# Seven products of quarters for the mixer's gate tiles in a float32 decoder step

## The chip, the cores and the metric

The kernel runs on one core of a Trainium2 chip. The metric is the device time of one execution in microseconds; the number for a kernel is the median of its runs.

## What is computed

One layer of a decoder over 560 token columns: 512 prompt tokens, 32 sampled tokens (8 sequences of 4) and 16 meta tokens. It is a feed-forward part, a mixer with two branches (gated linear attention and stick-breaking attention), and a second feed-forward part. The change is in the end of the mixer, cut here to what matters:

```python
u = rms_norm(h, mix_pre_g)
proj = u @ w_in                       # ..., r_a, q_b, k_b, v_b, gate_a, gate_b
o_a = rms_norm(o_a, gla_norm_g).reshape(B, L, V_GLA) * jax.nn.silu(r_a)
o_b = sb_attend(q_b, keys, vals, sb_bias, q_off).reshape(B, L, SB_W)
m = jax.nn.sigmoid(gate_a) * (o_a @ w_o_gla) + jax.nn.sigmoid(gate_b) * (o_b @ w_o_sb)
h = h + rms_norm(m @ w_out, mix_post_g)
```

All widths here are 1024, so each of `r_a`, `gate_a`, `gate_b` and the two output products has eight tiles of 128 output features. Everything is float32.

## The kernel before

Activations lie transposed: features on the 128 partitions, tokens along the free dimension, 544 tokens in this part, in two halves of 280 and 264 columns. A float32 product is made of float32r matmuls: an operand x is split into `hi`, its cast, and `lo`, x - hi, and a product takes three matmuls, hi·hi, hi·lo and lo·hi. A plain tile (`tile_steps`) goes over eight blocks of 128 input features and both halves of the tokens: 48 matmuls. After each six of them it yields once; such a step is the clock of the schedule.

Weights come by DMA in raw tiles of 128 x 1024 (three buffers). `split` has ScalarE cast one to `hi`, and `later(3, ...)` has VectorE subtract to `lo` three steps on (three buffers each). All vector subtractions and additions go through the one line L143. `later(n, f)` runs f after n more steps; `when` puts f at a given step. The order in which instructions are issued on TensorE, VectorE, ScalarE and GpSimd is that of the program, and each engine works through its own queue in that order. Temporary tiles come from an arena of 150 units of 280 columns (`take`, `give`), which reuses the room that has been free longest.

In the feed-forward parts most tile pairs (gate and up of one block of features) already take another form, `seven`: weights and activations are cut into quarters and the pair is made of seven products of quarters, after Strassen, instead of eight. Each product is 4 blocks x 3 matmuls of 272 columns, in all 84 matmuls and 14 steps. It takes four differences of weight quarters (`weight_sums`, 128x512), the parts of these (`parted`, `parted_lo`), four sums of activation quarters, made once, and five additions on the outputs.

In the mixer before, after the attention's own products, tiles follow each other in this order: r3 to r7 (`gate_r`, the silu gate of linear attention, whose results are split as they come), then for n = 0 to 7 an a tile (`gate_s`: the sigmoid of gate_a) and an o tile (`out_a`: o_a @ w_o_gla, multiplied by the sigmoid), then b0 to b7 (`gate_s` for gate_b), then p0 to p7 (o_b @ w_o_sb, `mixed`: times the sigmoid, plus m1, split for the next product), then the output projection m @ w_out, with halves of the tokens one after the other. Beside r3 to a4 run the products of the sampled tokens' attention; their last copies (`sample_out`) come at a4. The names and lines that matter below: `gate_s` L1940, `out_a` L1951, `names` L2067, `mixed` L2117, the loop over p L2144, the splits of the attention output at the second step of each b tile. At the start of each tile `ahead` splits the weights two tiles on and asks for a further raw tile; the hidden state, kept in DRAM meanwhile, is asked for at p1.

Of the kernel before, what the change touches and what calls it, by code (L numbers as in the profile page):

```python
# [8 lines left out]
F32 = mybir.dt.float32  # L9
# [6 lines left out]
P = 128  # L16
# [20 lines left out]
UP1 = (2, 5)  # L37
UP2 = (2, 5)
RE_FFN = 3
AHEAD = 150  # L40
SPREAD = 15
UNITS = 150
# [2 lines left out]
class Arena:  # L45
# [47 lines left out]
    def give(self, *aps):  # L93
        for a in aps:
            _, c, s, k = self.held.pop(id(a))
            self.clock += 1
            self.freed[c][s : s + k] = [self.clock] * k


class Parts:  # L100


    def __init__(self):
        self.t, self.rooms = {}, []

    def get(self, k, h, w):
        hi, lo = self.t[k, h]
# [4 lines left out]
def hybrid_step(  # L112
# [29 lines left out]
    def tt(out, a, b, op, eng=None):  # L142
        (eng or V).tensor_tensor(out=out, in0=a, in1=b, op=op)  # L143
# [683 lines left out]
    def gate_up_weights(plan, g_, u_, f0):  # L827
        for f in range(f0, KF):
            if f < RE_FFN or plan[f - RE_FFN] == "R":
                st.todo.extend((w, 0, KD, P * f, P, f < RE_FFN and "tile") for w in (g_, u_))  # L830
            else:
                st.todo.extend((w, r0, KD, P * f, P, "quarters") for w, r0 in (((g_, u_), 0), ((u_, g_), 4 * P)))

    def early_tiles(u, rs, wid, nw, hid, pairs, wait, prepare, first=False):

        early, held = {}, {}
# [39 lines left out]
    def other_tiles(old, gain, rs, nw, wid, hid, pairs, plan, late, sums_at, begun):  # L876
# [5 lines left out]
        QW = nw // 2  # L882
        QS = (slice(0, QW), slice(QW, nw))
        ub, sums = Parts(), {}
        pr_, ur, sr_, sp_ = {}, {}, {}, {}
        kinds = {RE_FFN + i: c for i, c in enumerate(plan)}
        start_, n = {}, 0
# [6 lines left out]
        def when(n, f, *args):  # L894
            at.setdefault(n, []).append((f, args))
# [59 lines left out]
            when(SP0 + SPE * i + 9, lambda i=i: give(pr_[i], pr_[i + 2]))  # L955


        quarters = {}

        def parted(f, key, src, room=None):  # L960

            count[0] += 1
            kt = src.shape[1]
            hi, lo = (sp.tile([P, KD, P], F32R, tag=t, name=f"{t}{count[0]}") for t in ("hi", "lo"))
            S.copy(hi[:, :kt], src)  # L965
            quarters[f, key] = hi, lo, src, room

        def parted_lo(f, key, more=False):
            hi, lo, src, room = quarters[f, key]
            tt(lo[:, : src.shape[1]], src, hi[:, : src.shape[1]].bitcast(F32), ALU.subtract)  # L970
            if room is not None:
                give(room)
            if more:
                st.fetch()

        def weight_sums(f, n):

            if n == 0:
                quarters[f] = st.raws.pop(0)[0], st.raws.pop(0)[0], take(KD * P), take(4 * P)
            r1, r2, t, t4 = quarters[f]  # L980
            t, t4 = (x.rearrange("p (k n) -> p k n", n=P) for x in (t, t4))
            b11, t1, b22, b21, t2, t3 = r1[:, :4], r1[:, 4:], r2[:, :4], r2[:, 4:], t[:, :4], t[:, 4:]
            tt(*((t3, b22, t1), (t1, t1, b11), (t2, b22, t1), (t4, b21, t2))[n], ALU.subtract)

        def parts_of(f, key):
            r1, r2, t, t4 = quarters[f]
            if key == "b1":
                parted(f, key, r1)
            elif key == "b2":
                parted(f, key, r2)  # L990
            elif key == "t":
                parted(f, key, t.rearrange("p (k n) -> p k n", n=P), t)
            else:
                parted(f, key, t4.rearrange("p (k n) -> p k n", n=P), t4)

        def raw_of(f, what):
            parted(f, what, st.raws.pop(0)[0])

        for f, c in kinds.items():
            n = start_[f]  # L1000
            if c == "S":
                for i, d in enumerate((-10, -10, -9, -8)):
                    when(n + d, weight_sums, f, i)
                for key, d, e in (("b1", -6, -5), ("t", -2, -1), ("b2", 0, 1), ("t4", 4, 6)):
                    when(n + d, parts_of, f, key)
                    when(n + e, parted_lo, f, key, key in ("b1", "b2"))
# [136 lines left out]
    st.todo += [(w, 0, KD, c + P * n, P, False) for n in range(8) for w, c in ((win, C_GA), (w_o_gla[0], 0))]  # L1143
    st.todo += [(win, 0, KD, C_GB + P * n, P, False) for n in range(8)]
    st.todo += [(w_o_sb[0], 0, KD, P * n, P, False) for n in range(8)]
# [4 lines left out]
    with tc.manual_schedule(engines={E.PE, E.DVE, E.Activation, E.Pool}):  # L1150
# [765 lines left out]
    def ahead():  # L1916
        st.split()
        st.fetch()
# [18 lines left out]
        later(2, by)  # L1937
        later(4, lambda: split(oas, n, o, oap))

    def gate_s(n, kept):  # L1940
        acc = yield from tile_steps(um, W1)
        sg = take(NW)
        kept.append(sg)

        def sig():
            for h in range(2):
                S.activation(sg[:, h * HW : h * HW + W2[h]], acc[h][:, : W2[h]], AF.Sigmoid)

        later(1, sig)

    def out_a(n):  # L1951
        acc = yield from tile_steps(oas, W1)

        def by():
            for h in range(2):
                c = slice(h * HW, h * HW + W2[h])
                tt(m1[n][:, c], acc[h][:, : W2[h]], m1[n][:, c], ALU.mult)

        later(1, by)

    def unwide():
        while wide:
# [23 lines left out]
    with tc.manual_schedule(engines={E.PE, E.DVE, E.Activation, E.Pool}):  # L1986
# [80 lines left out]
        names = [f"r{n}" for n in range(3, 8)] + [f"{c}{n}" for n in range(8) for c in "ao"] + [f"b{n}" for n in range(8)]  # L2067
        at = {}

        def when(t, n, f, *args):  # L2070

            at.setdefault(8 * names.index(t) + n, []).append((f, args))

        when("r4", 1, sample_new, 0)
        for i, t in enumerate(PAGES):
            if not t:
                continue
            what, c, b0 = t
            t = names[i]
            if what == "k":  # L2080
                for n, k in enumerate((1, 2, 5, 6)):
                    when(t, k, use_keys, b0, n)
                when(t, 9, sample_products, 1, b0, 0, kT, z)
                when(t, 9, sample_products, 1, b0, 1, kT, z)
            else:
                when(t, 1, use_values, c, b0)
            when(t, 7, ask)
        w1 = Weights(1)
        for n, f in w1.pieces(1):
            when("o1", n, f)  # L2090
        when("o1", 11, lambda: give(*qz, kns, z))
        when("a2", 5, sample_new, 1)
        t = names[len(PAGES)]
        when(t, 1, lambda: give(*ring))
        for n in range(4):
            when(t, 1 + 2 * n, sample_out, n)
        for n in range(8):
            when(f"b{n}", 2, lambda n=n: split(obs, n, ob[n], obp))
        mains = {f"r{n}": gate_r(n) for n in range(3, 8)}
        for n in range(8):  # L2100
            mains |= {f"a{n}": gate_s(n, m1), f"o{n}": out_a(n), f"b{n}": gate_s(n, sgb)}
        n = 0
        for t in names:
            ahead()
            for _ in mains[t]:
                n += 1
                step()
                for f, args in at.get(n, ()):
                    f(*args)
            if t == "o7":  # L2110
                later(1, lambda: give(*oap))
        for p in um.t.values():
            give(*p)

        ms, msp = Parts(), {}

        def mixed(n, acc):  # L2117
# [18 lines left out]
            for d, f in ((1, by), (2, lambda: tt(t, t, m1[n], ALU.add)), (3, hi), (5, lo)):  # L2136
                later(d, f)

        def product(act, hs, parts):
# [4 lines left out]
        for n in range(8):  # L2144
            ahead()
            if n == 1:
                hT[:], hT_room = whole(KD)
                for k in range(KD):
                    nc.sync.dma_start(hT[k], h_dram[k])
            mixed(n, product(obs, (0, 1), st.parts.pop(0)))  # L2150
        later(1, lambda: give(*obp))


        u2, rs2 = Parts(), take(NT)
        n2 = Gain(u2, g_pre2, rs2, W2)
# [94 lines left out]
```

## Time and profile before

| | us |
|---|---|
| median of 3 runs | 1536.91 |
| lowest and highest run | 1534.63, 1537.57 |
| span of the profiled execution | 1527.7 |
| TensorE busy | 1510.8 |
| VectorE busy | 966.6 |
| ScalarE busy | 726.9 |
| GpSimd busy | 149.0 |

The profile is one execution. It gives its span, from the first to the last instruction, and no time beside that; the median of the runs is 9.2 us longer than the span. PE is TensorE's matmuls, PEld its weight loads, DVE VectorE, ACT ScalarE, POOL GpSimd, SP the engine that issues the DMAs. A row of the timeline has the start in us from the span's start, the duration in us, the engine, the line, the operation, its output and input tiles, their shapes and how many instructions were merged; in brackets stands idle time ahead of it and what ended that. Matmuls overlap, so the duration of one is not the distance between two; that distance has to be read from starts. The gates and output products of the mixer lie between about 880 and 1085 us, the second feed-forward part's seven-product tiles from about 1165 us on.

### The profile page before, as it was taken

How to read it: one execution, taken by the hardware profiler on the slowest of the kernel's cores; microseconds unless marked ns; L12 is line 12 of the kernel's file. 1: busy time of each engine (PE TensorE's matmuls, PEld its weight loads, DVE VectorE, ACT ScalarE, POOL GpSimd, SP SyncE). 2: the span in 40 equal slices, each digit the busy share in tenths (PEclk: the TensorE clock that was granted, in tenths of full speed). 3: DMA queues.
4: the chain of work that ended last, by engine and by line, in shares of the span. 5: the costliest groups of instructions: out<-in, count | busy, mean ns of one | idle time of the engine just before them, and what ended most of it. 6: DMA issues, size and time to landing. Idle time of an engine off the chain costs nothing.

```text
span 1527.7 us, 29425 instructions
## 1 busy us (share of the span) xinstructions
PE 1510.8 (99%) x12059; PEld 1458.6 (95%) x12059; DVE 966.6 (63%) x1702; ACT 726.9 (48%) x1339; POOL 149.0 (10%) x216
## 2 busy tenths in 40 slices
PE   8999999999999999999999999999999999999998
PEld 7999999999999889999989999999999999999997
DVE  5788887423775756877777543224567898874234
ACT  6454444424555556565555432233465555543234
POOL 3000000000000011123324641000000000000000
PEclk9999999999999999999999999999999999999999
DMA  7233333524554363334445763442432333353243
GB/s 212 67 100 93 106 93 114 154 88 126 147 156 117 107 96 87 79 71 107 120 98 126 198 188 102 99 142 83 125 106 67 97 98 107 101 155 102 85 118 97
DMA packets 274647, 173.17 MB, mean 113 GB/s; under 512 B 9338, under 2 KB 263600, under 8 KB 274512
## 3 DMA queue, kind: packets, MB, share of 16 engines
q1 hardware_dynamic: 269072, 154.44, 37.7%
q0 software_dynamic: 5440, 16.85, 3.0%
q8 instruction: 95, 1.56, 0.4%
q14 instruction: 40, 0.33, 0.1%
HBM read 152.84 MB, written 18.42 MB: 112 GB/s over the span
## 4 chain that ended last, share of the span: by engine, by line
PE 96%; ACT 2%; DMA 1%; DVE 1%; issue 0%; SPq 0%
PE acc L680 11%; PE acc L681 10%; PE acc L683 10%; PE acc L667 9%; PE acc L670 8%; PE acc L668 8%; PE acc L1089 7%; PE acc L1090 7%; PE acc L1091 7%; PE acc L1029 2%; PE acc L1032 2%; PE acc L1030 2%; PE ps L1662 1%; PE ps L1646 1%; PE ps L1756 1%; PE ps L1561 1%
## 5 line engine op out<-in xcount | busy, mean ns | idle before, releaser
L143 DVE TENSOR_TENSOR lo<-raw,hi 128x1024 fp32r<-128x1024 f32 (+1 forms) x216 | 258.5, 1197 | 232.8 <-ACT hi L646 223.3
L667 PE MATMUL acc<-room,hi 128*128 128x280 f32 (+1 forms) x1024 | 297.2, 307 | 0.0
L143 DVE TENSOR_TENSOR room<-room,room 128x544 f32<-128x544 f32 (+15 forms) x340 | 221.3, 671 | 109.3 <-ACT room L724 55.9
L646 ACT CAST hi<-raw 128x1024 fp32r<-128x1024 f32 (+1 forms) x144 | 146.6, 1018 | 282.4 <-PE acc L681 158.5
L668 PE MATMUL acc<-room,hi 128*128 128x280 f32 (+1 forms) x1024 | 275.9, 289 | 0.0
L680 PE MATMUL acc<-room,hi 128*128 128x280 f32 (+1 forms) x912 | 256.5, 291 | 0.0
L681 PE MATMUL acc<-room,hi 128*128 128x280 f32 (+1 forms) x912 | 253.5, 289 | 0.0
L1090 PE MATMUL acc<-room,hi 128*128 128x280 f32 (+1 forms) x840 | 243.3, 290 | 0.0
L1089 PE MATMUL acc<-room,hi 128*128 128x280 f32 (+1 forms) x840 | 243.3, 290 | 0.0
L1091 PE MATMUL acc<-room,lo 128*128 128x280 f32 (+1 forms) x840 | 243.0, 289 | 0.0
L683 PE MATMUL acc<-room,lo 128*128 128x280 f32 (+1 forms) x912 | 218.9, 290 | 0.0
L670 PE MATMUL acc<-room,lo 128*128 128x280 f32 (+1 forms) x1024 | 212.5, 289 | 0.0
L667 PEld LDWEIGHTS acc<-room,hi 128*128 128x128 f32 x1024 | 193.0, 188 | 12.2 <-issue 10.7
L668 PEld LDWEIGHTS acc<-room,hi 128*128 128x128 f32 x1024 | 193.2, 189 | 2.8 <-issue 1.9
L680 PEld LDWEIGHTS acc<-room,hi 128*128 128x128 f32 x912 | 171.6, 188 | 2.1 <-issue 0.9
L681 PEld LDWEIGHTS acc<-room,hi 128*128 128x128 f32 x912 | 171.6, 188 | 0.2
L670 PEld LDWEIGHTS acc<-room,lo 128*128 128x128 f32 x1024 | 159.7, 188 | 0.0
L1091 PEld LDWEIGHTS acc<-room,lo 128*128 128x128 f32 x840 | 158.1, 188 | 0.0
L1089 PEld LDWEIGHTS acc<-room,hi 128*128 128x128 f32 x840 | 158.0, 188 | 0.0
L1090 PEld LDWEIGHTS acc<-room,hi 128*128 128x128 f32 x840 | 157.9, 188 | 0.0
L683 PEld LDWEIGHTS acc<-room,lo 128*128 128x128 f32 x912 | 153.9, 188 | 0.0
L965 ACT CAST hi<-raw 128x1024 fp32r<-128x1024 f32 x72 | 75.3, 1052 | 83.8 <-PE acc L1090 48.3
(333 smaller groups left out, 2560.3 us busy)
## 6 DMA issues: line engine op xcount, KB each, us to landing
raw<-in_w_in_dram SPq DMA_DIRECT2D x63, 512.0 KB, 7.4
raw<-in_ffn_w_down_dram SPq DMA_DIRECT2D x42, 448.0 KB, 3.5
raw<-in_ffn_w_gate_dram SPq DMA_DIRECT2D x60, 256.0 KB, 3.2
raw<-in_ffn_w_up_dram SPq DMA_DIRECT2D x60, 256.0 KB, 3.4
raw<-in_ffn_w_down_dram SPq DMA_DIRECT2D x21, 512.0 KB, 3.6
out_dram<-room SPq DMA_DIRECT2D x32, 256.0 KB, 3.0
raw<-in_ffn_w_gate_dram SPq DMA_DIRECT2D x14, 512.0 KB, 3.9
raw<-in_ffn_w_up_dram SPq DMA_DIRECT2D x14, 512.0 KB, 3.9
```

What stands on the lines that cost most here:

```text
L143: (eng or V).tensor_tensor(out=out, in0=a, in1=b, op=op)
L646: S.copy(h_, src)
L667: T.matmul(acc[h][:, : wid[h]], hi[k], a[h][0], start=(k == 0), stop=False)
L668: T.matmul(acc[h][:, : wid[h]], hi[k], a[h][1], start=False, stop=False)
L670: T.matmul(acc[h][:, : wid[h]], lo[k], a[h][0], start=False, stop=(k == KD - 1))
L680: T.matmul(acc[h][:nw, : wid[h]], wh, a[h][0], start=(k == 0), stop=False)
L681: T.matmul(acc[h][:nw, : wid[h]], wh, a[h][1], start=False, stop=False)
L683: T.matmul(acc[h][:nw, : wid[h]], wl, a[h][0], start=False, stop=(k == kt - 1))
L965: S.copy(hi[:, :kt], src)
L1089: T.matmul(x[:, :QW], hi, act[k][0], start=(first and k == 0), stop=False, skip_group_check=True)
L1090: T.matmul(x[:, :QW], hi, act[k][1], start=False, stop=False, skip_group_check=True)
L1091: T.matmul(x[:, :QW], lo, act[k][0], start=False, stop=(k == 3), skip_group_check=True)
```

## The change

Fourteen of the sixteen tiles of gate_a and gate_b become seven pairs in the seven-product form: b0 (with b1), a2, b2, a4, b4, a6, b6. Tiles a0 and a1 stay plain. The eight o tiles move ahead of all gates: they now follow r7 directly and ScalarE copies them to `m1` as they are; the gates multiply `m1` later. The p tiles are put between the gate pairs.

The input u of the gates, until now two halves of tokens per block of features, is held in whole tiles (`um.full`, the same room in all), so that quarters can be cut from it. Its four quarter sums are made from o7's seventh step on, in four blocks, one every four steps: `whole_u` adds hi and lo again (two additions of 544 columns), `u_sums` makes four sums of 272 columns, `u_hi` casts and `u_lo` subtracts (two of 544 each). The splits of the attention output move from the b tiles to b0's second step and every fourth step from there. The helpers of the seven-product form (`parted`, `parted_lo`, `weight_sums`, `parts_of`) move out of the feed-forward part unchanged.

The weights of a plain tile are split five steps before it, not two tiles before. At the end of the mixer the first set of the output projection is split five steps and the second one step before the end of p7. The hidden state is asked for in p6 instead of p1.

```diff
+MIXER = [("R", "r", n) for n in range(3, 8)]
+MIXER += [("R", "o", n) for n in range(8)] + [("R", "a", 0), ("R", "a", 1), ("S", "b", 0), ("S", "a", 2), ("S", "b", 2), ("R", "p", 0), ("R", "p", 1)]
+MIXER += [("S", "a", 4), ("R", "p", 2), ("R", "p", 3), ("S", "b", 4), ("S", "a", 6), ("R", "p", 4), ("R", "p", 5), ("S", "b", 6)]
+MIXER += [("R", "p", 6), ("R", "p", 7)]
...
+    def weights_at(when, n, f):
+        for i, d in enumerate((-10, -10, -9, -8)):
+            when(n + d, weight_sums, f, i)
+        for key, d, e in (("b1", -6, -5), ("t", -2, -1), ("b2", 0, 1), ("t4", 4, 6)):
+            when(n + d, parts_of, f, key)
+            when(n + e, parted_lo, f, key, key in ("b1", "b2"))
+
+    def seven_steps(f, act, qw, outs):
...
+        for n, g in ((3, lambda: copied("e1", a)), (5, lambda: copied("e5", d)), (7, lambda: add("u2", "e1", b)),
+                     (9, lambda: add("v", "e5", c)), (10, lambda: made("c22", "u2", o["v"][:, :qw], "v")),
+                     (11, lambda: outs["c11"](a[:, :qw])), (13, lambda: made("c12", "u2", d[:, :qw])),
+                     (15, lambda: made("c21", "u2", c[:, :qw], "u2"))):
+            later(n, g)
+        for x, act_, key, k0, first in ((a, a11, "b1", 0, True), (d, s1, "b1", 4, True), (b, s2, "t", 0, True), (c, s3, "t", 4, True),
+                                        (a, a12, "b2", 4, False), (d, s4, "b2", 0, False), (c, a22, "t4", 0, False)):
+            for k in range(4):
+                hi, lo = (t[:, k0 + k] for t in quarters[f, key][:2])
+                T.matmul(x[:, :qw], hi, act_[k][0], start=(first and k == 0), stop=False, skip_group_check=True)
+                T.matmul(x[:, :qw], hi, act_[k][1], start=False, stop=False, skip_group_check=True)
+                T.matmul(x[:, :qw], lo, act_[k][0], start=False, stop=(k == 3), skip_group_check=True)
+                if k % 2:
+                    yield
...
         def mix_tile(h, k):
-            hi, lo = um.t[k, h] = (take(HW, F32R), take(HW, F32R))
+            if h == 0:
+                um.full[k] = take(NT, F32R), take(NT, F32R)
+                for i in range(2):
+                    um.t[k, i] = um.full[k][0][:, cs[i]], um.full[k][1][:, cs[i]]
+            hi, lo = um.t[k, h]
...
+    def whole_u(i):
+        half_made["x"] = x, y = take(NT), take(NT)
+        for t, k in ((x, i), (y, i + 4)):
+            hi, lo = um.full[k]
+            tt(t[:, :NW], hi[:, :NW].bitcast(F32), lo[:, :NW].bitcast(F32), ALU.add)
...
+    def u_sums(i):
+        x, y = half_made.pop("x")
+        half_made["s"] = sa, sb = take(NT), take(NT)
+        q0, q1 = slice(0, QW), slice(QW, NW)
+        tt(sa[:, q0], x[:, q1], y[:, q1], ALU.add)
+        tt(sb[:, q0], x[:, q0], x[:, q1], ALU.subtract)
+        tt(sa[:, q1], sa[:, q0], x[:, q0], ALU.subtract)
+        tt(sb[:, q1], y[:, q0], sa[:, q1], ALU.subtract)
...
     def out_a(n):
         acc = yield from tile_steps(oas, W1)
...
-                tt(m1[n][:, c], acc[h][:, : W2[h]], m1[n][:, c], ALU.mult)
+                S.copy(m1[n][:, h * HW : h * HW + W2[h]], acc[h][:, : W2[h]])
...
+        for i, (kind, what, t) in enumerate(MIXER):
+            starts[what, t] = n
+            if kind == "S":
+                weights_at(when, n, (what, t))
+            elif i > 1:
+                when(n - 5, st.split)
+                when(n - 4, st.fetch)
+            n += 14 if kind == "S" else 8
+        for d in (-5, -1):
+            when(n + d, st.split)
+            when(n + d + 1, st.fetch)
+        for i in range(4):
+            for j, f in enumerate((whole_u, u_sums, u_hi, u_lo)):
+                when(starts["o", 7] + 7 + 4 * i + (0, 1, 3, 5)[j], f, i)
+        for i in range(8):
+            when(starts["b", 0] + 2 + 4 * i, lambda i=i: split(obs, i, ob[i], obp))
...
+        when(starts["p", 6] + 2, h_back)
```

More of the change, by code (lines that the diff above doesn't have):

```diff
@@ L2137, in mixed, with product_b, h_back @@
                 later(d, f)
+        def product_b(n):
+            acc = yield from tile_steps(obs, W1)
+            mixed(n, acc)
+        starts, n = {}, 0
+        for i, (kind, what, t) in enumerate(MIXER):
[9 more added lines that the diff above has]
+            when(n + d + 1, st.fetch)
+        for i in range(4):
+            for j, f in enumerate((whole_u, u_sums, u_hi, u_lo)):
+                when(starts["o", 7] + 7 + 4 * i + (0, 1, 3, 5)[j], f, i)
+        for i in range(8):
+            when(starts["b", 0] + 2 + 4 * i, lambda i=i: split(obs, i, ob[i], obp))
+        def h_back():
+            hT[:], hT_room_[:] = whole(KD)
+            for k in range(KD):
+                nc.sync.dma_start(hT[k], h_dram[k])
+        hT_room_ = []
+        when(starts["p", 6] + 2, h_back)
+        mains = {"r": gate_r, "o": out_a, "p": product_b, "a": gate_a}
+        n = 0
+        for kind, what, t in MIXER:
+            for _ in mains[what](t) if kind == "R" else gate_pair(what, t):
+                n += 1
+                step()
+                for f, args in at.pop(n, ()):
+                    f(*args)
+            if (what, t) == ("o", 7):
+                later(1, lambda: give(*oap))
+            if (what, t) == ("b", 6):
+                later(1, lambda: give(*kept_sums, *(t for p in um.full.values() for t in p)))
+        assert not at, sorted(at)
+        hT_room = hT_room_
+        later(1, lambda: give(*obp))
         def product(act, hs, parts):
@@ L2142, in product @@
             return acc
[L2144 to L2151, printed above, removed]
         u2, rs2 = Parts(), take(NT)
```

190 lines of the change are left out of this document (111 added, 79 removed).

## The prediction

> **What bounds the kernel now.** I read the page first, then the busy times by stretch, then the order of single instructions at four places. The page says that TensorE is the bound:
>
> ```profile
> span 1527.7 us, 29425 instructions
> PE 1510.8 (99%) x12059; PEld 1458.6 (95%) x12059; DVE 966.6 (63%) x1702; ACT 726.9 (48%) x1339; POOL 149.0 (10%) x216
> PE 96%; ACT 2%; DMA 1%; DVE 1%; issue 0%; SPq 0%
> ```
>
> TensorE is busy for all but 17 us and carries 96% of the chain that ended last, so a matmul that is taken away shortens the span unless something else becomes late. The next question is how much room the other engines have where the change is made. The stretches below answer it: two from the mixer's gates and output products, two from the second feed-forward part, whose tiles already have the form that the gates are to get. Columns after the stretch: its length, then busy time of PE, PEld, DVE, ACT, POOL, then TensorE's granted clock, DMA share, GB/s.
>
> ```profile
> 965.00:990.00 25.00, 25.00 (x201) 25.00 (x200) 7.18 (x10) 6.25 (x9) 0.00 (x0) 1.00 0.51 90
> 1015.00:1040.00 25.00, 25.00 (x202) 25.00 (x201) 7.95 (x9) 8.49 (x16) 0.00 (x0) 1.00 0.29 85
> 1215.00:1240.00 25.00, 25.00 (x202) 25.00 (x201) 22.82 (x36) 13.53 (x21) 0.00 (x0) 1.00 0.30 86
> 1265.00:1290.00 25.00, 25.00 (x202) 25.00 (x201) 22.37 (x36) 12.20 (x19) 0.00 (x0) 1.00 0.36 106
> ```
>
> In the mixer VectorE works 7 to 8 of 25 us; under seven-product tiles it works 22.4 to 22.8, about 90%, with TensorE still never idle. So the form itself can be fed, but it leaves VectorE only a tenth of its time, and whatever the change adds on top must fit there.
>
> **The matmuls that go.** A plain tile is 48 matmuls; its weights' low part (the 128x1024 subtraction) comes once per tile, so two neighbours give the period. A seven-product tile is 84 matmuls and replaces two plain tiles; its period is read between the same weight difference of two neighbours.
>
> ```profile
> 1002.23 1.22 DVE L143 TENSOR_TENSOR lo<-raw,hi 128x1024 fp32r<-128x1024 f32 x1 [4.17 <-ACT hi L646]
> ...
> 1008.26 1.23 DVE L143 TENSOR_TENSOR lo<-raw,hi 128x1024 fp32r<-128x1024 f32 x1 [4.17 <-ACT hi L646]
> ```
>
> ```profile
> 1222.22 0.72 DVE L143 TENSOR_TENSOR room<-room,room 128x544 f32<-128x544 f32 x1
> 1222.86 0.68 DVE L143 TENSOR_TENSOR room<-raw,raw 128x512 f32<-128x512 f32 x1
> 1223.58 0.69 DVE L143 TENSOR_TENSOR raw<-raw 128x512 f32<-128x512 f32 x1
> 1224.30 0.69 DVE L143 TENSOR_TENSOR room<-raw,raw 128x512 f32<-128x512 f32 x1
> 1224.91 0.72 DVE L143 TENSOR_TENSOR room<-room,room 128x544 fp32r<-128x544 f32 x1
> 1225.55 0.69 DVE L143 TENSOR_TENSOR lo<-room,hi 128x512 fp32r<-128x512 f32 x1
> 1226.15 0.69 DVE L143 TENSOR_TENSOR room<-raw,room 128x512 f32<-128x512 f32 x1
> 1226.75 0.78 DVE L143 TENSOR_TENSOR room<-room,acc 128x272 f32<-128x272 f32 x2
> 1227.45 1.22 DVE L143 TENSOR_TENSOR lo<-raw,hi 128x1024 fp32r<-128x1024 f32 x1
> 1228.58 0.44 DVE L143 TENSOR_TENSOR room<-room 128x272 f32<-128x272 f32 x1
> ...
> 1234.81 0.69 DVE L143 TENSOR_TENSOR room<-raw,raw 128x512 f32<-128x512 f32 x1
> ```
>
> 1008.26 - 1002.23 = 6.03 us per plain tile, so 0.754 us per step of six matmuls, the unit in which the kernel places its side work. 1234.81 - 1224.30 = 10.51 us per seven-product tile, 0.125 us per matmul. Sixteen gate tiles cost 16 x 6.03 = 96.5 us now. Afterwards two stay plain and seven pairs take 7 x 10.51: 12.06 + 73.57 = 85.6 us. The change removes 84 matmuls and **10.9 us** of TensorE time. The reordering (all eight output tiles of linear attention first, gated later) moves matmuls but keeps their number.
>
> **What VectorE gets instead.** The same rows give what an instruction takes in a full queue (start to next start): 0.64 us for 544 columns, 1.13 (1228.58 - 1227.45), call it 1.14, for 1024, 0.60 for 512, and 0.72 where the next one reads its result, so 0.11 more. For 272 columns I take 0.44 - 0.09 = 0.35, since the 512 forms overlap by that 0.09.
>
> The critical place is the sums of the mixer's input. They must be there for the first seven-product pair, b0, but begin only at step 7 of the last output tile, o7, so they have a tile's last step and the two plain gates a0 and a1 to hide under. There are four blocks. Each takes two whole additions (0.64 + 0.75), four half sums (0.35 + 0.35 + 0.46 + 0.35, the third read at once by the fourth) and two low parts (1.28): 4.18 us, together 16.7. TensorE waits first for the fourth block's first low part, so 0.64 less counts: 16.1 us. VectorE takes them in program order, with other work between: a1's weight low part 1.14, b0's four weight differences 0.72 + 0.72 + 0.60 + 0.60, the gating of m1 by a0 0.64, two low parts of b0's weights 2.28, and the sixteen small copies of the sampled attention, 3.22:
>
> ```profile
> 949.42 3.22 DVE L1892 COPY room<-ps 64x32 f32<-64x32 f32 x16 [0.65 <-PE ps L1884]
> ```
>
> That is 9.9, so VectorE has 26.0 us of work before TensorE can do the last quarter of b0's second product. When does it start? Its queue stands behind the low part of a0's weights, which waits for ScalarE's cast, which waits for ScalarE's two copies out of o6, which need o6 to be done:
>
> ```profile
> 995.12 1.05 ACT L646 CAST hi<-raw 128x1024 fp32r<-128x1024 f32 x1 [4.42 <-PE acc L668]
> ...
> 996.07 0.68 ACT L1947 ACTIVATE room<-acc 128x280 f32<-128x280 f32 x2
> ...
> 996.20 1.23 DVE L143 TENSOR_TENSOR lo<-raw,hi 128x1024 fp32r<-128x1024 f32 x1 [4.17 <-ACT hi L646]
> ...
> 996.63 0.65 ACT L1908 CAST room<-room 128x544 fp32r<-128x544 f32 x1
> ```
>
> From o6's end: 0.08 to begin, two evictions 0.56 (996.63 - 996.07), the cast 1.05, the low part 1.14 with 0.03 between: 2.9 us, which is 3.2 us before a0 begins. TensorE, unhindered, reaches the waiting matmul after a0 and a1 (12.06) and 22 matmuls of b0 (2.75), 14.8 us after a0 begins. So VectorE has 18.0 us for 26.0: TensorE waits **8.0 us**, about 1.4 of it for b0's first weights and the rest in one piece before that quarter. Bounds: nothing, if the sums hid as the feed-forward part's own sums do; 10.4, if the queue reached the sums only when TensorE reached their place in the program (2.4 us later). I take 8.0, since each term has its row. Behind the late low part stand b0's second weights, the gating by a1, and the splits of the attention output, one 0.64 every four steps. From there to the end of b2 VectorE has the weight work of two pairs (each four differences 2.64 and low parts 3 x 1.14 + 0.60, so 13.3), the outputs of three (five 272-column instructions each, 5.4), eight splits 5.1, the gating by a1 and a2 1.9, and three low parts that are left over, 2.9: 28.6 us. TensorE still has 38 steps, 28.7 us. So VectorE stays full and TensorE gets nothing back; one more wait of 0.6 at a2's first weights is possible.
>
> A wait that long also costs clock. At the start of the run TensorE sat idle once for 2.67 us:
>
> ```profile
> 21.90 0.63 PE L1236 MATMUL ps<-room,ones 128*128 128x128 f32 x2 [2.67 <-DVE room L1235]
> 20.50:25.00 4.50, 3.10 (x15) 3.04 (x15) 2.26 (x6) 1.93 (x5) 0.00 (x0) 0.67 0.42 124
> ```
>
> and the granted clock of the stretch fell to 0.67. That is 4.5 x 0.33 = **1.5 us** of matmul time lost, which I add for the 6.6 us wait; it also hides the 0.6 at a2. Bounds: nothing, and twice that. [...]
>
> The other pairs do not meet the input's sums. Between them stand plain products (a6 follows b4 directly), so VectorE is at or below the 90% of the feed-forward rows: nothing. The first output tile now follows its last input r7 without the tile that stood between; its eighth step comes 5.3 us after r7, where product, cast and low part need about 3: nothing, at most a step.
>
> **The end of the mixer.** The output weights were split a whole tile ahead; now the second set is split in the last step of the last product, and its low parts land between two instructions of the chain that makes the last mixed tile. That chain already makes TensorE wait:
>
> ```profile
> 1085.46 0.29 PE L680 MATMUL acc<-room,room 128*128 128x280 f32 x1
> 1085.54 0.79 DVE L143 TENSOR_TENSOR room<-acc,room 128x280 f32<-128x280 f32 x2 [2.63 <-PE acc L683]
> 1086.36 0.73 DVE L143 TENSOR_TENSOR room<-room,room 128x544 f32<-128x544 f32 x1
> 1087.00 1.29 DVE L143 TENSOR_TENSOR room<-raw,room 128x512 fp32r<-128x512 f32 x2
> 1088.21 0.72 DVE L143 TENSOR_TENSOR room<-room,room 128x544 fp32r<-128x544 f32 x1
> 1088.98 0.40 PE L681 MATMUL acc<-room,room 128*128 128x280 f32 x1 [0.53 <-DVE room L143]
> ```
>
> A second pair of 128x512 instructions in front costs 1.21 (1088.21 - 1087.00) more: **+1.2 us**, at most 2.4 if the reload of the hidden state, which moves from the second product to the seventh and goes out on the same queue, also holds the third set back. The reload itself is due only after eight more half tiles: nothing.
>
> **The sum.** -10.9 + 8.0 + 1.5 + 1.2 = -0.2 us. Unknown and on one side only are waits for reused rooms (the sums hold 32 units more; bounds: nothing, and one 1.14 low part each at one or two places); I add 0.7. So +0.5 on the profiled 1527.7. The page gives no time around the span; the median of the runs, 1536.91, is 9.2 above it, and I keep that difference: **1537.5 us**. Of the 10.9 saved almost all is given back at one place. A measurement of this kernel can tell about 0.2%, 3.1 us, from no change; this is inside.
>
> **Rivals.** *Faster: the sums hide.* If VectorE's queue gets ahead by another plain tile, or the half sums overlap more than the lone 0.44 row lets me say, the wait at b0 halves to 4 and stays in pieces under the 2.67 us that cost the clock. Then -10.9 + 4 + 1.2 = -5.7: 1531. Fully hidden it is -9.7: 1527. For it: the feed-forward sums are hidden in the trace. Against: those have tens of us, these have 18.
>
> *Slower: the second quarter tile is late.* A seven-product tile needs two raw tiles, and the second can be fetched only when the low part of the previous pair's first weights frees a buffer, 17.5 steps ahead; the first difference is due 10 steps ahead, so 7.5 steps or 5.7 us remain. The transfers:
>
> ```profile
> raw<-in_ffn_w_gate_dram SPq DMA_DIRECT2D x30, 256.0 KB, 3.2
> raw<-in_ffn_w_up_dram SPq DMA_DIRECT2D x30, 256.0 KB, 3.4
> ...
> raw<-in_w_in_dram SPq DMA_DIRECT2D x12, 512.0 KB, 7.7
> ```
>
> The feed-forward halves land in time; 512 KB of the input projection took 7.7 us, 2.0 too long. VectorE would stand in its queue for 2.0 us with everything behind it. In a6 it has 10.51 - 22.37/25 x 10.51 = 1.1 us to spare and TensorE loses 0.9; in a2 and b2 the splits have used that up and it loses 2.0 each: +4.9, so 1542. It decides once the second raw tile lands more than 5.7 us after it is asked for. Against it: the first difference needs only the first half of the second raw tile.
>
> *That TensorE's work does not shrink* has no ground: the number of matmuls is fixed by the code.
>
> **How the numbers follow.** The forecast, 1534 to 1541 around 1537.5 (its terms' bounds without both extremes at once), gets 0.50, of which 0.42 lies within 0.2% and 0.08 above; the faster rival 0.20; the slower one 0.30. So faster 0.20, same 0.42, slower 0.38. The range takes in the slower rival with 2.5 us more for rooms and the halved wait of the faster one: 1531 to 1545; outside remain the fully hidden sums and a pile-up of both delays.
>
> **What would show it.** Right: 84 matmuls fewer; at the first pair one TensorE wait of 6 to 7 us on VectorE and a stretch of clock below 1; VectorE full for about 45 us from the end of o7; a wait near 1.9 us on VectorE at the first output-projection tile; other pairs at 10.5 us. Wrong: no wait over 3 us at b0 (faster), VectorE itself waiting for DMA before weight differences (the slower rival), or waits spread over the later pairs.

## The result and the profile after

The changed kernel takes 1535.99 us (median of 12 runs, 1534.16 to 1537.84), the kernel before 1535.70 (12 runs, 1533.91 to 1537.57): ratio 1.0002, interval 0.9994 to 1.0011. No difference can be told. The forecast was 1537.5.

The page of the changed kernel (span; busy time of each engine; the chain that ended last):

```profile
span 1534.7 us, 29467 instructions
PE 1509.2 (98%) x11975; PEld 1454.8 (95%) x11975; DVE 1027.2 (67%) x1803; ACT 752.7 (49%) x1384; POOL 148.5 (10%) x216
PE 92%; DVE 3%; ACT 3%; DMA 1%; issue 1%; SPq 0%; DVEq 0%; ACTq 0%
```

12059 - 11975 = 84 matmuls are gone, and VectorE has 60.6 us more to do. Where TensorE then stands still shows in the list of its waits from 940 to 1100 us of the changed kernel (operation and what it waited for: us in total, times, longest):

```profile
PE acc L915 <- DVE room L147: 4.5, 1, 4.5
PE acc L914 <- ACT room L2053: 1.6, 1, 1.6
PE acc L685 <- DVE room L147: 0.7, 1, 0.7
PE acc L684 <- ACT room L2220: 0.6, 1, 0.6
```

The first two stand in one place, the fourth block of b0's second product, the lower two at the first half tile of the output projection. In the kernel before the same stretch has one wait, 0.5, at the output projection. The stretches that answer to those shown of before (same columns):

```profile
955.00:980.00 25.00, 18.92 (x130) 18.40 (x129) 24.56 (x53) 11.37 (x19) 0.00 (x0) 0.86 0.21 60
980.00:1005.00 25.00, 25.00 (x201) 25.00 (x201) 21.16 (x33) 14.83 (x25) 0.00 (x0) 1.00 0.41 106
1005.00:1030.00 25.00, 25.00 (x201) 25.00 (x200) 19.31 (x30) 9.98 (x14) 0.00 (x0) 1.00 0.36 96
```

At b0 VectorE is busy 24.56 of 25 us, TensorE 18.92, and the granted clock is 0.86; from 980 us on TensorE is busy throughout again. VectorE's timeline and TensorE's two waits show the same place instruction by instruction:

```profile
942.43 0.72 DVE L147 TENSOR_TENSOR room<-room 128x544 f32<-128x544 f32 x1
...
948.17 1.71 DVE L147 TENSOR_TENSOR room<-room,room 128x544 fp32r<-128x544 f32 x3 [1.46 <-ACT room L2053]
...
964.69 3.25 DVE L1946 COPY room<-ps 64x32 f32<-64x32 f32 x16
967.97 1.22 DVE L147 TENSOR_TENSOR lo<-room,hi 128x1024 fp32r<-128x1024 f32 x1
969.11 1.35 DVE L147 TENSOR_TENSOR room<-room,room 128x544 fp32r<-128x544 f32 x2
```

```profile
965.03 0.39 PE L914 MATMUL acc<-room,hi 128*128 128x272 f32 x1 [1.62 <-ACT room L2053]
969.88 0.59 PE L915 MATMUL acc<-room,hi 128*128 128x272 f32 x1 [4.46 <-DVE room L147]
```

The last low part of the quarter sums runs from 969.11, two instructions merged; after the first of them TensorE goes on, at 969.88. Just ahead of it, with one weight low part between, stand the sixteen copies of the sampled attention, 3.25 us. TensorE needs these only in p0, three pairs on, by way of the splits of the attention output.

**A warning on this profile.** Its span is 7.0 us longer than that of before, and that is not the change. The products of values gathered for the sampled tokens (before: L1856) run ahead of the gates. The groups of instructions, first the kernel before, then the changed one, then the changed one in a repeat (e5, below):

```profile
L1856 PE MATMUL ps<-room,room 128*32 128x128 f32 x256 | 8.5, 274 | 0.0
```

```profile
L1910 PE MATMUL ps<-room,room 128*32 128x128 f32 x244 | 11.5, 285 | 4.1 <-issue 4.0
```

```profile
L1910 PE MATMUL ps<-room,room 128*32 128x128 f32 x244 | 8.6, 274 | 0.0
```

11.5 + 4.1 - 8.6 = 7.0 us. The profiled execution took 1536.38, 1.7 above its span. By the same 1.7 the profile of before was an execution of about 1529.4, which none of the 12 timed runs of before was (1533.91 the lowest). So that profile seems to have been taken where these products are fast and the timed runs where they are slow; no profile of the kernel before shows them slow. The shift is about the same for both kernels: beside the experiments below, which ran on three chips, the kernel before took 1528.1 to 1528.3, 7.4 to 7.6 less, and the changed one 1528.71, 7.3 less.

### The profile page after: what moved, and what is told of

It is laid out like the page before. It is cut to its first block, busy times and chain, and to the rows that moved or that the text cites. A ratio compares the mean times of both kernels' runs of the same rounds, so it can differ in the third digit from the quotient of the medians.

```text
span 1534.7 us, 29467 instructions
## 1 busy us (share of the span) xinstructions
PE 1509.2 (98%) x11975; PEld 1454.8 (95%) x11975; DVE 1027.2 (67%) x1803; ACT 752.7 (49%) x1384; POOL 148.5 (10%) x216
## 4 chain that ended last, share of the span: by engine, by line
PE 92%; DVE 3%; ACT 3%; DMA 1%; issue 1%; SPq 0%; DVEq 0%; ACTq 0%
PE acc L684 9%; PE acc L685 9%; PE acc L687 9%; PE acc L671 8%; PE acc L674 7%; PE acc L672 7%; PE acc L1134 7%; PE acc L1135 7%; PE acc L1136 7%; PE acc L1074 2%; PE acc L1075 2%; PE acc L1077 2%; DVE room L147 2%; PE acc L915 2%; PE acc L916 2%; PE acc L914 2%
## 5 line engine op out<-in xcount | busy, mean ns | idle before, releaser
L147 DVE TENSOR_TENSOR room<-room,room 128x544 fp32r<-128x544 f32 (+16 forms) x365 | 234.7, 665 | 121.0 <-ACT room L728 56.9
L671 PE MATMUL acc<-room,hi 128*128 128x280 f32 (+1 forms) x928 | 271.9, 310 | 0.0
L672 PE MATMUL acc<-room,hi 128*128 128x280 f32 (+1 forms) x928 | 250.8, 289 | 0.0
L1134 PE MATMUL acc<-room,hi 128*128 128x280 f32 (+1 forms) x840 | 243.6, 290 | 0.0
L1135 PE MATMUL acc<-room,hi 128*128 128x280 f32 (+1 forms) x840 | 243.4, 290 | 0.0
L1136 PE MATMUL acc<-room,lo 128*128 128x280 f32 (+1 forms) x840 | 243.2, 289 | 0.0
L684 PE MATMUL acc<-room,hi 128*128 128x280 f32 (+1 forms) x784 | 221.9, 292 | 0.0
L685 PE MATMUL acc<-room,hi 128*128 128x280 f32 (+1 forms) x784 | 219.2, 290 | 0.0
L650 ACT CAST hi<-raw 128x1024 fp32r<-128x1024 f32 (+1 forms) x130 | 131.9, 1015 | 152.8 <-PE acc L685 139.5
L674 PE MATMUL acc<-room,lo 128*128 128x280 f32 (+1 forms) x928 | 193.2, 289 | 0.0
L687 PE MATMUL acc<-room,lo 128*128 128x280 f32 (+1 forms) x784 | 192.6, 290 | 0.0
L671 PEld LDWEIGHTS acc<-room,hi 128*128 128x128 f32 x928 | 175.2, 189 | 12.4 <-issue 10.9
L672 PEld LDWEIGHTS acc<-room,hi 128*128 128x128 f32 x928 | 175.6, 189 | 2.8 <-issue 1.9
L1134 PEld LDWEIGHTS acc<-room,hi 128*128 128x128 f32 x840 | 158.2, 188 | 0.0
L1136 PEld LDWEIGHTS acc<-room,lo 128*128 128x128 f32 x840 | 158.2, 188 | 0.0
L1135 PEld LDWEIGHTS acc<-room,hi 128*128 128x128 f32 x840 | 157.9, 188 | 0.0
L684 PEld LDWEIGHTS acc<-room,hi 128*128 128x128 f32 x784 | 147.6, 188 | 2.1 <-issue 0.9
L685 PEld LDWEIGHTS acc<-room,hi 128*128 128x128 f32 x784 | 147.5, 188 | 0.2
L674 PEld LDWEIGHTS acc<-room,lo 128*128 128x128 f32 x928 | 145.2, 188 | 0.0
L845 ACT CAST hi<-raw 128x1024 fp32r<-128x1024 f32 x86 | 90.1, 1053 | 107.7 <-PE acc L1135 48.2
L687 PEld LDWEIGHTS acc<-room,lo 128*128 128x128 f32 x784 | 134.1, 188 | 0.0
```

The lines of the kernel that those rows point to most:

```text
L650: S.copy(h_, src)
L671: T.matmul(acc[h][:, : wid[h]], hi[k], a[h][0], start=(k == 0), stop=False)
L672: T.matmul(acc[h][:, : wid[h]], hi[k], a[h][1], start=False, stop=False)
L674: T.matmul(acc[h][:, : wid[h]], lo[k], a[h][0], start=False, stop=(k == KD - 1))
L684: T.matmul(acc[h][:nw, : wid[h]], wh, a[h][0], start=(k == 0), stop=False)
L685: T.matmul(acc[h][:nw, : wid[h]], wh, a[h][1], start=False, stop=False)
```

## The experiments

**The same two kernels again** (e1: the kernel before unchanged; e5: the changed kernel unchanged), to see which of the differences between the profiles belong to the change.

> The kernel before, once more, for a second profile and the clocks of more runs. The first profile of the changed kernel lost 7.1 us against that of the kernel before in the four products of the sampled values that stand before the gates (12.1 us of matmul time where 4.0 would do with clock, waits that the profile puts down to nothing). Theory A: these waits come and go from run to run and have nothing to do with the change; then this profile shows them too, or part of them, its span is nearer to 1534 than to 1527.7, and the ratio is 1.000. Rival B: the new order of tiles makes them; then this profile has 0.99 us for each of the four and a span of 1528 again.

> The changed kernel once more, beside the others on one chip, as the base for them. Theory A (the four products of sampled values lost time by the chip, not by the order of tiles): 0.99 us for each of the four as in the kernel before, span about 1528, ratio 1.000; the wait at b0 as in the first profile, 1.6 and 4.5 us, and one stretch of half clock after it. Rival B (the order of tiles makes those waits): 2 us or more for each, span 7 us over that of the kernel before.

e1 took 1528.36 us, ratio 0.9997 (0.9987 to 1.0006) to itself; e5 took 1528.71, ratio 1.0004 (0.9995 to 1.0013). e1 shows no waits at these products and a span of 1527.5, which by the letter is the sign of its rival; e5 refutes that rival: the changed kernel is without them too (last row above), so the order of tiles does not make them. The waits at b0 are back to within 0.02 us. TensorE's timeline of e5 at b0's first matmul, at the long wait, and at the first matmuls of p0, of a4 and of b4:

```profile
951.77 0.29 PE L914 MATMUL acc<-room,hi 128*128 128x272 f32 x1
...
961.19 0.59 PE L915 MATMUL acc<-room,hi 128*128 128x272 f32 x1 [4.46 <-DVE room L147]
...
992.38 0.29 PE L671 MATMUL acc<-room,hi 128*128 128x280 f32 x1
...
1004.42 0.30 PE L914 MATMUL acc<-room,hi 128*128 128x272 f32 x1
...
1027.01 0.30 PE L914 MATMUL acc<-room,hi 128*128 128x272 f32 x1
```

b0, a2 and b2 take 992.38 - 951.77 = 40.6 us. The plain p0 and p1 take 1004.42 - 992.38 = 12.04, so a4 takes 1027.01 - 1004.42 - 12.04 = 10.55: three clean pairs would be 31.6, and the place costs **9.0 us** of the 7 x 1.5 = 10.5 that the seven pairs save. At 10.55 / 84 = 0.1256 us per matmul the 22 matmuls ahead of the one at 961.19 take 2.8, so TensorE is 6.7 late there (the two waits of 1.6 and 4.5, and 0.6 around them); the 230 matmuls from there to p0 take 31.2 instead of 28.9, so another 2.3 come behind the wait.

**No quarter sums** (e2). This kernel leaves out the sums, with their casts on ScalarE and their low parts; its products take quarters of the input itself, so only its time is of use.

```diff
 def whole_u(i):
-    ... two additions of 544
+    ... takes the input's hi and lo as they are
 def u_sums(i):
-    ... four sums of 272
+    usum["s", 2 * m + h, i] = usum["a", h, i + 4 * m]
 def u_hi(i): / def u_lo(i):
-    ... two casts, two subtractions of 544
+    pass
```

> The changed kernel without the quarter sums of the mixer's input (no whole additions, no half sums, no casts and low parts of them; the products take quarters of the input itself, so the outputs are not the reference's). Theory A (the saving is given back at the first pair, where TensorE waits for these sums): no wait at b0 beyond 0.5 us, no drop of the clock there, time 8 to 9 us under the changed kernel, ratio to the kernel before about 0.9945. Rival B (the seven-product tiles of the mixer lose the time elsewhere, in late weights or in the output chain): the time stays within 2 us of the changed kernel, ratio 0.999 to 1.000.

1518.61 us, ratio 0.9937 (0.9921 to 0.9952). The stretch of e2, and its list of waits from 940 to 1100 us:

```profile
955.00:980.00 25.00, 25.00 (x200) 24.82 (x199) 24.23 (x38) 16.26 (x28) 0.00 (x0) 1.00 0.35 95
```

```profile
PE acc L685 <- DVE room L147: 0.8, 1, 0.8
PE acc L684 <- ACT room L2204: 0.6, 1, 0.6
```

Without the sums nothing waits at b0, and the kernel is 9.6 us faster than before: 10.5 for the matmuls less 1.1 at the output projection (worked out below, under the end of the mixer) would be 9.4. Apart from that 1.1, the missing gain lies in the sums of the input.

**Is the lost clock a cost of its own?** In e3 and e6 TensorE does 40 or 28 needless float32 products of 128 columns while it would wait, to keep its clock up.

```diff
+if (f, k) == (("b", 0), 3) and x is d and first:
+    p = ps()
+    for _ in range(40):        # 28 in e6
+        T.matmul(p[:, :P], ones, ones, start=True, stop=True)
```

> The changed kernel with 40 matmuls of 128 columns on constants put in front of the matmul of b0 that waits, so that TensorE works through most of the wait (about 4.7 us). Theory A (the wait also costs clock: 4 us at half clock after it, 2 us of matmul time): the granted clock stays at 1.00 in that stretch, b0 to the end of b2 takes 2 us less, ratio to the kernel before 0.9985 to 0.999. Rival B (the time after the wait is set by VectorE, which is full, so the clock does not matter): clock 1.00, but TensorE waits for VectorE a little later instead, ratio as for the changed kernel, 1.000.

> As the earlier kernel with constants multiplied during the wait, but with 28 instead of 40 (0.221 us each, 6.2 us), so that they end before the quarter sums are there at 6.6 us: in the earlier one they took 8.85 us and held TensorE 2.2 us too long, while the rest of b0, a2 and b2 took 2.2 us less than at half clock. Theory A (the clock after the wait costs 2.2 us): b0 to the end of b2 takes 38.4 us instead of 40.6, ratio 0.9985. Rival B (VectorE, full, makes up for it): a new wait on VectorE in a2 or b2 and 40 us or more.

e3: 1527.53 us, ratio 0.9995 (0.9986 to 1.0004). e6: 1529.10, ratio 1.0005 (0.9996 to 1.0014). The clock is 1.00 in both from 955 to 980 us, where it is 0.86 in e5. In e3 the 40 products end 2.2 us after the sums are ready, so its time says little by itself. The 28 of e6 end before; these are the stretch and the rows of its TensorE timeline at b0's first matmul, at the one that waits for the sums, at two later waits and at p0's first matmul:

```profile
955.00:980.00 25.00, 23.67 (x193) 23.24 (x192) 24.13 (x49) 13.92 (x25) 0.00 (x0) 1.00 0.34 79
```

```profile
953.41 0.29 PE L918 MATMUL acc<-room,hi 128*128 128x272 f32 x1
...
962.83 0.39 PE L919 MATMUL acc<-room,hi 128*128 128x272 f32 x1
...
970.58 0.39 PE L918 MATMUL acc<-room,hi 128*128 128x272 f32 x1 [1.22 <-DVE room L147]
...
981.75 0.39 PE L918 MATMUL acc<-room,hi 128*128 128x272 f32 x1 [0.35 <-DVE room L147]
...
993.88 0.29 PE L671 MATMUL acc<-room,hi 128*128 128x280 f32 x1
```

40.5 us from b0 to p0, as without the warm products (40.6). From the matmul that waits for the sums to p0, e5 takes 992.38 - 961.19 = 31.2 us with the lowered clock, and e6 takes 993.88 - 962.83 = 31.1 at full clock: there TensorE catches up with VectorE and waits for it again, 1.22 and 0.35. So behind the sums either of the two, the clock or the full VectorE, holds TensorE back by a good 2 us. They lie over each other, and to take away the clock's part alone gains nothing.

**The whole additions on GpSimd** (e7), which takes 8 of VectorE's additions away.

```diff
-tt(t[:, :NW], hi[:, :NW].bitcast(F32), lo[:, :NW].bitcast(F32), ALU.add)
+tt(t[:, :NW], hi[:, :NW].bitcast(F32), lo[:, :NW].bitcast(F32), ALU.add, G)
```

> The changed kernel with the eight whole additions of hi and lo on GpSimd instead of VectorE. Theory A (VectorE's queue ahead of the last quarter sum sets the wait): VectorE has 5.6 us less before it, the wait at b0 falls from 6.1 to about 1 us, the clock does not drop, time 6 to 7 us under the changed kernel, ratio 0.9955. Rival B (GpSimd takes so long for an addition, over 2 us, or slows VectorE beside it, that the sums come no earlier): the wait stays over 4 us, ratio over 0.9985.

1531.07 us, ratio 1.0018 (1.0009 to 1.0027): slower than before. GpSimd's and VectorE's timelines of e7, the last row being the same three instructions with GpSimd quiet:

```profile
939.70 3.76 POOL L147 TENSOR_TENSOR room<-room 128x544 f32<-128x544 f32 x2 [1.59 <-PE ps L1910]
```

```profile
939.71 4.05 DVE L147 TENSOR_TENSOR room<-room,room 128x544 fp32r<-128x544 f32 x3 [4.12 <-ACT room L2053]
...
955.68 1.70 DVE L147 TENSOR_TENSOR room<-room,room 128x544 fp32r<-128x544 f32 x3
```

An addition that took VectorE 0.64 takes GpSimd 1.9 here, and for as long VectorE's three instructions take 4.05 instead of 1.70. Most of the 5.6 that VectorE is spared it loses in speed: 2.35 in this row and 2.3 in two later ones (1.85 instead of 0.69 and 2.87 instead of 1.70). And it stands still for 4.12 us ahead of this row, for ScalarE's cast, where the changed kernel has 1.46. The waits at b0 become 3.2 and 3.7.

**The sixteen copies on ScalarE** (e11), nothing else.

```diff
-V.tensor_copy(ob[pr][r_, NP : NP + NS]...
+S.copy(ob[pr][r_, NP : NP + NS]...
```

> The changed kernel (seven pairs) with only the sixteen small copies, 3.25 us of VectorE's queue before the last quarter sum, on ScalarE. Theory A (VectorE's queue sets both the wait and what follows it): from b0 to the end of b2 37.4 us instead of 40.6, 3.2 us less, ratio 0.998 to 0.9985. Rival B (ScalarE, which then has the casts behind the copies, becomes the late one, or the clock after the wait sets the time): 39.5 us or more, ratio 0.9995 or more.

1526.65 us, ratio 0.9992 (0.9983 to 1.0001). b0 to p0 is 38.2 us instead of 40.6: 2.4 come back of the 3.2 that VectorE is spared. The time alone would not tell e11 from the kernel before. Its first matmuls of b0 and p0, and its list of waits at b0:

```profile
952.92 0.29 PE L914 MATMUL acc<-room,hi 128*128 128x272 f32 x1
...
991.12 0.29 PE L671 MATMUL acc<-room,hi 128*128 128x280 f32 x1
```

```profile
PE acc L914 <- ACT room L2053: 1.6, 1, 1.6
PE acc L914 <- ACT room L2000: 1.5, 1, 1.5
PE acc L915 <- DVE room L147: 1.2, 1, 1.2
```

The wait for VectorE falls from 4.5 to 1.2, and a new one of 1.5 comes for ScalarE, whose sigmoid of a1's output (L2000) now stands behind the last of the sixteen. Nearer to the full gain than to none, and in part a wait handed on.

**One more plain pair ahead of b0** (e8: a2 and a3 plain, six pairs left), and with it the blocks of sums eight steps apart instead of four (e9).

```diff
-("R", "a", 0), ("R", "a", 1), ("S", "b", 0), ("S", "a", 2), ("S", "b", 2)
+("R", "a", 0), ("R", "a", 1), ("R", "a", 2), ("R", "a", 3), ("S", "b", 0), ("S", "b", 2)
# e9 also:
-when(starts["o", 7] + 7 + 4 * i + ...
+when(starts["o", 7] + 7 + 8 * i + ...
```

> The changed kernel with the pair a2 as two plain tiles, put ahead of b0: six pairs instead of seven (1.5 us more matmul time), but two tiles, 12.1 us, more under which the quarter sums can hide. Theory A (only the lack of cover before the first pair costs): no wait over 0.5 us at b0, no drop of the clock, 9.1 - 1.5 = 7.6 us under the changed kernel, ratio 0.995. Rival B (VectorE stays full through the pairs whatever comes before them): waits on VectorE move into b0 and b2 and the gain is under 3 us, ratio 0.998 or more.

> The kernel with a2 and a3 plain, with a block of quarter sums every eight steps instead of every four. In that kernel TensorE still waited 2.67 us, now in the plain tile a2, because the low part of its weights stood behind the sums in VectorE's queue (954.12, after the tile had begun), and the clock fell once. Theory A (it is the order and the cover of VectorE's queue, nothing in the products): with the sums spread no TensorE wait over 0.5 us up to the end of b2, clock 1.00, b0 and b2 21.0 us, 4 us under that kernel, ratio 0.995. Rival B (VectorE's total work is too much even so): a wait of 2 us or more moves into b0, ratio 0.997 or more.

e8: 1524.30 us, ratio 0.9977 (0.9968 to 0.9986). e9: 1525.07, ratio 0.998 (0.9971 to 0.9989). Both beat the kernel before although they save 12 matmuls fewer than the change; neither came to the 0.995 that was expected. The waits before and in the pairs, e8 first, then e9; then the stretch of e8 at its wait:

```profile
PE acc L674 <- DVE lo L147: 2.7, 1, 2.7
```

```profile
PE acc L914 <- DVE room L147: 1.3, 1, 1.3
PE acc L916 <- DVE lo L147: 1.2, 1, 1.2
...
PE acc L674 <- DVE lo L147: 0.6, 1, 0.6
```

```profile
950.00:960.00 10.00, 7.33 (x47) 7.12 (x46) 9.68 (x27) 2.71 (x5) 0.00 (x0) 0.83 0.32 44
```

In e8 the sums are ready in time for b0, but the wait has moved ahead into the plain a2, whose own low part stands in VectorE's queue behind them. The terms: -6 x 1.5 for the matmuls, +2.7 for the wait, +1.7 for the clock (10 x 0.17; here nothing hides it: b0 and b2 behind it run clean, 21.0 us, and from the last product of the sampled values to b0 the starts are 4.4 us longer than e5's and two plain tiles), +1.1 at the output projection: -3.5, and -3.8 was measured (2.1 to 4.9 by the interval). Spread wider (e9), the sums make three short waits (1.3, 1.2 and 0.6) and no loss of clock (1.00 from 950 to 980 us), but come later: the sum of VectorE's work has not changed, and the time is no better than e8's.

**These put together** (e10: e9, the copies of e11, and the output projection's weights of e4, which follows).

> The same with spread sums, the weight sets of the output projection four steps earlier and the sixteen small copies of the sampled attention on ScalarE. Theory A: 1 us more from the output projection and nothing from the copies, since nothing waits for VectorE there any more: ratio 0.9943. Rival B (waits at b0 remain, so the copies count): 2 to 4 us more than with spread sums alone.

1519.37 us (5 runs), ratio **0.9941** (0.9927 to 0.9954): faster than both kernels. All its waits from 940 to 1100 us, and the stretch:

```profile
PE acc L914 <- DVE room L147: 0.7, 1, 0.7
PE acc L685 <- DVE room L147: 0.5, 1, 0.5
```

```profile
955.00:980.00 25.00, 24.26 (x194) 24.04 (x193) 23.79 (x37) 14.66 (x25) 0.00 (x0) 1.00 0.35 94
```

Six pairs save 9.0 us; from b0 to p0 the starts are 1.0 longer than two clean pairs (the wait of 0.7 with it); so 8.0 was to be expected, and 8.9 was measured (7.0 to 11.2 by the interval). It is 5.7 under e9 by the medians, and the starts of the two traces place 3.9 of it: 0.8 ahead of b0, 2.0 from b0 to p0, 1.1 at the output projection. So waits at b0 had remained in e9 and the copies counted, as the rival of the expectation had it. The two profiled executions are e9's fastest (1523.91) and e10's slowest (1520.86); the part of the 5.7 that the traces do not place stays open. e9 itself should be 4.1 under the kernel before by its starts; 3.2 was measured (1.7 to 4.4), so nothing is clearly missing there. No run has e8 with the copies on ScalarE and the sums not spread, so it is not shown that the spreading helps at all.

**The output projection's weights earlier** (e4).

```diff
-        for d in (-5, -1):
+        for d in (-9, -5):
```

> The changed kernel with the first two weight sets of the output projection split four steps earlier (nine and five steps before the end of the mixer instead of five and one). Theory A (the second set's low parts stand between two instructions of the last mixed tile's chain and cost 1.2 us): the wait at the first output-projection tile falls from 1.3 us to about 0.5, as in the kernel before, and the time by 1 us, ratio to the kernel before about 0.9995. Rival B (the chain waits on ScalarE or the third set anyway): the wait stays over 1 us and the time does not move.

1527.08 us, ratio 0.9995 (0.9986 to 1.0004). The wait of 0.6 + 0.7 becomes 0.53, as in the kernel before:

```profile
1088.16 0.40 PE L685 MATMUL acc<-room,room 128*128 128x280 f32 x1 [0.53 <-DVE room L147]
```

The trace shows the mechanism; about 1 us is too little for the time to show it.

## Why the prediction came out right, step by step

**The matmuls.** 84 fewer, and 10.5 us where 10.9 was forecast.

**The wait at b0.** Forecast: VectorE has 26.0 us of work and 18.0 of cover, so TensorE is 8.0 late. Measured: 27.4 and 20.7, so 6.7 late. VectorE's chain from the first addition to the low part that TensorE waits for lasted from 942.43 to 969.83; the difference to 26.0 is the 1.46 for ScalarE's cast in the rows above. The cover is longer by a term that the prediction left out, the last two products of the sampled values, one of which runs inside o7 and one inside a0:

```profile
940.41 1.08 PE L1910 MATMUL ps<-room,room 128*32 128x128 f32 x32
...
947.63 0.43 PE L1910 MATMUL ps<-room,room 128*32 128x128 f32 x8
...
948.64 0.39 PE L671 MATMUL acc<-room,hi 128*128 128x280 f32 x1
```

With them o7 and a0 take 7.2 us each instead of 6.0, and a1, in which four transposes run, takes 6.5. Two errors of opposite sign thus left the sum near. TensorE waits there in two pieces, 1.62 and 4.46, where the forecast had about 1.4 for b0's first weights and the rest in one piece; the first piece was not for b0's weights but for ScalarE's cast of the quarter sums.

**The clock.** Here the forecast was wrong in kind. The clock fell (0.86 in the stretch), and in e8 (0.83 over 10 us), where the pairs behind the wait have slack, that costs its price, an estimated 1.7 us. At b0 it is no cost of its own, as e6 showed. The prediction had put VectorE's work behind the wait level with TensorE's (28.6 us against 28.7) and so at no cost, with one more wait of 0.6 under the clock. In e6, at full clock, VectorE holds TensorE back by 31.1 - 28.9 = 2.2 there, as much as the clock does without the warm products (2.3). The 1.5 for the clock stands where VectorE's pace would have to stand. Wait and what follows it were forecast at 9.5; the place costs 9.0.

**One reading of the rows.** The prediction puts 0.72 between 128x512 instructions down to the next one reading the result. That holds for 1223.58 to 1224.30; the one from 1222.86, 0.72 too, is followed by an instruction that overwrites its input instead. The sum is not touched.

**VectorE full, other pairs free.** Right: VectorE is busy 42.5 of the 45 us from 942 on, 24.56 of 25 at b0 and 21.16 in the next stretch; and a4 takes 10.55.

**The end of the mixer.** Forecast 1.2 more; the waits went from 0.53 to 1.32, 0.8 more, and the starts of the first two half tiles of the output projection moved apart from 3.89 to 4.96 us, by 1.1. In e4 they are 3.89 apart again, which confirms the cause.

**Rooms.** Forecast 0.7; TensorE's four waits between 940 and 1100 us are accounted for by other causes, so nothing is seen of it.

**The slower rival** (the second quarter tile late) exists, at 0.7 us: VectorE's waits from 970 to 1100 us hold

```profile
DVE room L147 <- DMA raw<-in_w_in_dram: 0.7, 2, 0.4
```

where 2.0 in each of three tiles was its condition. **The faster rival** needed the sums to hide; e2 shows what that would have been worth, and e8 and e10 that it takes other work ahead of b0 to hide most of it.

**The 9.2 us around the span.** That the absolute time came out right here was luck. The time around the span is 1.7; the rest would be the slow products of gathered values, in the timed runs of both kernels and not in the profile of before. Their nearly equal size in both kernels is why keeping the difference worked. The balance of the terms, -10.5 + 9.0 + 1.1 = -0.4 us, is what was forecast in substance: almost all is given back at one place.

## What to carry to other kernels

When a change saves work on the bound engine by giving a helper more, add up the helper's whole queue before the first use of its results, in program order, with whatever stands between, and compare it with the work the bound engine has in hand until then. If it does not fit, give the helper cover with tiles that do not need the results (e8), or take unrelated work off its queue to an engine that is free (e11); together, with the sums spread and the output projection's weights earlier, these turned a gain of nothing into 9 us (e10). The loss of clock after a wait counted in full in e8, an estimated 1.7 us (10 x 0.17), where nothing else was late behind it; at b0 it did not, since there VectorE holds TensorE back by 2.2 us at full clock as well (e6).

## What the hardware did that was not expected

- Beside two additions on GpSimd, 3.76 us in all, three of VectorE's took 4.05 us, and 1.70 with GpSimd quiet (e7). By what the one holds up the other, the trace does not show.
- After a single wait of 2.67 us the clock was 0.83 over 10 us (e8). It was 0.83 over 10 us too, in the first profile of the changed kernel, around four waits of 0.29 to 0.99 us, 2.05 in all, whose last is shown; e5, without them, has 1.00 in that stretch:

```profile
852.26 1.12 PE L1910 MATMUL ps<-room,room 128*32 128x128 f32 x16 [0.99 <-issue]
```

```profile
848.00:858.00 10.00, 7.95 (x77) 6.30 (x70) 3.97 (x6) 0.78 (x2) 6.75 (x7) 0.83 0.48 168
```

- The kernel before took 1535.70 us when it was first measured and 1528.1 to 1528.3 beside the experiments. The two profiles of the changed kernel, 1534.7 and 1525.9 us of span, differ by 7.0 us in products that read gathered values alone. What makes these slow is not known.
